# Hybrid S5 and attention encoder block: x and the result moved by position in the chunk, small vectors issued behind the weights

## Chip, cores and metric

The kernel runs on one core of a Trainium2 chip. The metric is device time in microseconds (us) of one execution; the runs of a kernel are told by their median. The profile is one further execution, recorded by the hardware profiler. Engines: PE multiplies matrices, DVE and POOL work elementwise, ACT evaluates functions and copies, and SP issues the transfers (DMA).

## The reference

One layer is computed for a prompt of 512 tokens and a sample of 256, with the same weights:

```
x += 1/2 * postnorm(SwiGLU_1(prenorm(x)))
h  = prenorm(x); z = h @ w_in  -> [u_ssm | q_c | kv_c | k_rope]
y_ssm = groupnorm(S5 bidirectional complex-diagonal SSM(u_ssm) + GLU)
y_att = groupnorm(bidirectional MLA(q_c, kv_c, k_rope))
x += postnorm(concat(y_ssm, y_att) @ w_out)
x += 1/2 * postnorm(SwiGLU_2(prenorm(x)))
```

The model width is 1024, the hidden width 2816, everything in float32. `g_q`, `g_ssm_out`, `b_glu` and `g_att_out` are the small vectors of the mixers.

## The kernel before

The 768 tokens are six tiles of 128. The state-space part works in chunks of 8 tokens, so the kernel keeps tokens in the order of the position j in the chunk: a tile of the prompt (tiles 0 to 3) holds two positions of 64 chunks each, a tile of the sample (4 and 5) four positions of 32 chunks. `runs` (L123) describes such a tile in DRAM, `load_x` (L128) loads it and `store_x` (L132) stores one of the result.

The stages, with the names that the prediction uses:

- **Start** (`run`, `read` L1144, `feed` L1152). Each tile of x is loaded, squared and summed on ACT (`squares`, L151), turned into a factor on POOL (L145, L146), normalised on DVE (L169) and turned by 8 PE transposes (L180); ACT and DVE split the columns into a high and a low part (L92, L93), the blocks B. The first products of the gate weights (L111 to L113, 24 to a group) need the three tiles of the first half of the tokens. `in_order` holds each engine to the order in which this is written.
- **First half-step**, with the state-space setup in the background, up to some 600 us.
- **Way out of the half-step** (`rows` L188, called by `out1` L1169). It takes a tile per step. The tile's row sum of squares (ACT) gives the factor r; DVE scales the tile (L211), POOL adds the residual tile x to it (L212), which `load_x` fetches again, and the sum is stored in a DRAM buffer, x1D. In the next step DVE scales the sum again for the next norm (L215), PE turns it, and so on. Steps are three deep, and each engine is held to the written order: on DVE a step is L211, L215, the two splits, and the two sums of products (L445).
- **Mixers** (`mix` L702): input projection, states, attention.
- **Way out of the mixers** (`mix_out` L1054): the same `rows`, with the residual read from x1D, whose rows lie in the order of the tile, and its result written to x2D.
- **Second half-step and its way out** (`out2` L1174): `rows` again without a next norm, the residual from x2D; `store_x` writes the result, the last tile in two halves of its channels (L232, L233).

All transfers are issued by SP, in one order that the tile scheduler sets. They take eight completion semaphores in turn, so that a transfer is issued when the one eight places before it has landed; a store also waits for the engine that makes its tile, and a load for its buffer.

Of the kernel before, what the change touches and what calls it, by code (L numbers as in the profile page):

```python
# [13 lines left out]
PSUM = bass.MemoryType.PSUM  # L14
# [4 lines left out]
NJ = 8  # L19
# [5 lines left out]
# Tokens lie in the order n = j*64 + k for the j-th token of the prompt's chunk k, then  # L25
# n = 512 + j*32 + k for the sample's. A chunk is 8 tokens.
# [3 lines left out]
# A float32 operand of a matmul is the exact sum of two float32r parts of 12 significant bits;  # L30
# a product is three passes, hi*hi + hi*lo + lo*hi.
#
# Half-step, per pair of 128-wide tiles of the hidden layer: with the weights' blocks A[tile][half
# of the inner dimension] and the tokens' blocks B[half of the inner dimension][half of the tokens],
# the four products of blocks take Winograd's seven multiplications.
# [6 lines left out]
PACE = 1.9  # steps of the setup in the background of each group of products  # L42
BACK = 27  # the unit of attention from which the states' way back goes beside it
WOUT = (35, 36, 37, 38)  # the units at which a row of blocks of w_out is made ready
AHEAD = 3  # how many of its matrices are loaded ahead
# [3 lines left out]
class Kernel:  # L49
# [17 lines left out]
    def load(self, src, shape, name="raw", tile=None):  # L67
        t = (tile or self.w4)(name, shape, F32)
        self.nc.sync.dma_start(t, src)
        return t  # L70

# [3 lines left out]
    # banks of PSUM: 4 for products, 2 for what follows them, 2 that serve a third purpose  # L75
# [19 lines left out]
    def opnd(self, src, eng=None):  # L95
        """[128, 4, 128] of weights as (hi, lo)"""
        t = self.w4("w", [2, 4, 128])
        self.split(t[:, 0], t[:, 1], src, eng)
        return t[:, 0], t[:, 1]

    def wrow(self, src):
        """[128, 1024] of weights as (hi, lo)"""
        h, l = (self.w4("w", [1024]) for _ in range(2))
        self.split(h, l, src)
        return h, l

    def prod(self, ps, A, B, start, stop):
        """ps (+)= A^T B over the four inner tiles of a block"""
        for k in range(4):
            first = start and k == 0  # L110
            self.nc.tensor.matmul(ps, A[0][:, k, :], B[0][:, k, :], start=first, stop=False, skip_group_check=True)  # L111
            self.nc.tensor.matmul(ps, A[0][:, k, :], B[1][:, k, :], start=False, stop=False, skip_group_check=True)  # L112
            self.nc.tensor.matmul(ps, A[1][:, k, :], B[0][:, k, :], start=False, stop=stop and k == 3, skip_group_check=True)  # L113

    def chain(self, ps, pairs):
        """ps = sum over (lhs hi, lhs lo, rhs hi, rhs lo)"""
        for i, (lh, ll, rh, rl) in enumerate(pairs):
            last = i == len(pairs) - 1
            self.nc.tensor.matmul(ps, lh, rh, start=i == 0, stop=False)  # L119
            self.nc.tensor.matmul(ps, lh, rl, start=False, stop=False)  # L120
            self.nc.tensor.matmul(ps, ll, rh, start=False, stop=last)  # L121

    def runs(self, x, t, drams):  # L123
        """the rows of a token tile in DRAM and in x, as [j, chunk, channel]"""
        which, n, j0 = (0, 2, 2 * t) if t < 4 else (1, 4, 4 * t - 16)
        return drams[which][0].rearrange("(k j) d -> j k d", j=NJ)[j0 : j0 + n], x

    def load_x(self, x, t, drams):  # L128
        src, dst = self.runs(x, t, drams)
        self.nc.sync.dma_start(dst, src)  # L130

    def store_x(self, drams, x, t, ch):  # L132
        dst, src = self.runs(x, t, drams)
        self.nc.sync.dma_start(dst[:, :, ch], src)
# [19 lines left out]
    def rms_cols(self, S, n, name):  # L154
        """one factor per token, [128, 6], from sums of squares [128 channels, 768 tokens]"""
        nc = self.nc
        ps = self.dn([128, 8], "ps_r")
        for t in range(NTILE):
            nc.tensor.matmul(ps[:, t : t + 1], S[:, 128 * t : 128 * t + 128], self.ones, start=True, stop=True)
        r = self.small.tile([128, NTILE], F32, name=name)  # L160
        nc.vector.tensor_scalar(r, ps[:, :NTILE], 1.0 / n, EPS, op0=ALU.mult, op1=ALU.add)
        nc.gpsimd.tensor_tensor(r, r, self.mhalf.broadcast_to([128, NTILE]), op=ALU.pow)
        return r

# [1 line left out]
    def normed(self, xn, x, g, spare):  # L166
        """xn = the normalised rows x"""
        r = self.rms_factor([self.sumsq(x, spare)], D)
        self.nc.vector.scalar_tensor_tensor(xn, x, r, g, op0=ALU.mult, op1=ALU.mult)  # L169

    def turn(self, xn, t, bl, bank=None):
        """the rows of a token tile as columns of the blocks bl; returns what takes them out of PSUM"""
        nh, c = t // 3, slice(128 * (t % 3), 128 * (t % 3) + 128)
        banks = []
# [13 lines left out]
    def rows(self, acc, produce, g_post, residual, store, g_pre=None, bl=None):  # L188
        """a sub-layer's way out by tiles of tokens: the last of its products, post-norm and residual, then the
        next one's pre-norm into the blocks bl; in steps, each tile three steps deep. Without a next one, the last  # L190
        tile goes by halves of its channels"""
# [48 lines left out]
    def in_order(self):  # L240
        """each engine takes what is traced here in that order"""
        traced = self.nc.cur_bb.bb.instructions
        n = len(traced)
# [9 lines left out]
    def combos(self, bl, out):  # L253
        """Winograd's sums of the tokens' blocks, in steps"""
# [33 lines left out]
    def group(self, last, calls):  # L288
        """the matmuls of an accumulation group, after the group that was last in its bank"""
# [7 lines left out]
    def behind(self, steps, count=1):  # L297
        """count of steps, their instructions kept behind those that each engine has been given before"""
# [15 lines left out]
    def ffn(self, bl, wnames, way_out, n_plain, feed, lead, background=iter(()), read=lambda nh: None):  # L314
# [6 lines left out]
        # at the start of the kernel GpSimd takes a share  # L321
# [185 lines left out]
    def cmul(self, t, o, a, b, eng):  # L507
        """o = a * b for pairs (re, im); t: a temporary of o's shape"""
# [7 lines left out]
    def ssm_setup(self):  # L516
# [43 lines left out]
        # the angle less its whole turns, in pieces of 2 pi whose products with the turns are exact  # L560
# [22 lines left out]
        # f = (lam_bar - 1) / lam  # L583
# [22 lines left out]
        # the states are kept conjugate, so that a real part is a sum of products  # L606
# [8 lines left out]
        # powers by offset: the forward half 1, lam .. lam^8; the backward half lam^8 .. lam, 1 from offset 1  # L615
# [82 lines left out]
    def chunks(self, dram):  # L698
        """[channels, tokens] as (first chunk, [j, c, g, k]) of the prompt and of the sample"""
        return [(k0, dram[:, a:b].rearrange("(g c) (j k) -> j c g k", c=16, j=NJ)) for k0, a, b in ((0, 0, 512), (64, 512, 768))]  # L700

    def mix(self, bl, before):  # L702
# [6 lines left out]
        def columns(c0, n, tile=self.w4):  # L709
            """n <= 2 tiles of 128 columns of w_in from c0, one at a time"""  # L710
# [3 lines left out]
        def from_h(op, i, nh, done):  # L714
            """their products: done(i, half, psum [128, 384])"""
# [5 lines left out]
        # the state-space inputs u, by way of DRAM to [(j, c), g, chunk]  # L721
# [28 lines left out]
        # chunk inputs of the states: column s of XS gets what enters the state after its chunk s-1,  # L750
        # the backward half in the reversed order of chunks
# [34 lines left out]
        # the queries' latents, times their gain; their norm is a factor per token  # L786
        gq = self.small.tile([128, 3], F32, name="gq")
        nc.sync.dma_start(gq, A["g_q"][0].rearrange("(t p) -> p t", p=128))
# [16 lines left out]
        # keys' and values' latents and the shared rotary key, token by token  # L805
# [29 lines left out]
        # projections of the queries, keys and values  # L835
# [5 lines left out]
        for k in range(3):  # L841
            raw = self.load(A["w_uq"][0, 128 * k : 128 * k + 128, :].rearrange("p (h d) -> p h d", h=8), [8, 96])
            h, l = (self.w4("w", [768]) for _ in range(2))
            # the halves of the rotary channels apart
# [58 lines left out]
        # what the states' way back reads  # L903
# [12 lines left out]
        # attention, by tiles of 128 queries  # L916
        cols = {}
        for nm in ("g_ssm_out", "b_glu"):
            cols[nm] = self.small.tile([128, 4], F32, name=nm)
            nc.sync.dma_start(cols[nm], A[nm][0].rearrange("(t p) -> p t", p=128))  # L920
# [3 lines left out]
        self.bcast(g_att, "g_att_out")  # L924
        # [half of the tokens][hi, lo]
# [8 lines left out]
        # in stages, each some units behind the one before: a unit is a tile of queries with one or two heads  # L934
# [24 lines left out]
        def weigh(u):  # L959
# [10 lines left out]
            if h0 + n == 8:  # L970
# [4 lines left out]
                # the group norm's factor goes with the rows of w_out's product  # L975
# [25 lines left out]
        def ssm_out():  # L1001
            for b in range(AHEAD):
                fetch(b)
            # the backward half back into the order of chunks
# [8 lines left out]
            for b in range(8):  # L1013
# [9 lines left out]
                # twice the tanh-gelu  # L1023
# [30 lines left out]
    def mix_out(self, ohl, ra, cols, wo, res, out_x2, bl):  # L1054
# [31 lines left out]
        for ct in range(4):  # L1086
# [9 lines left out]
            # from the order by j and the chunks of both sequences to that of the tokens  # L1096
# [97 lines left out]
def constants():  # L1194
    """what depends on shapes alone: the identity, rotary tables by position, a diagonal mask"""
# [36 lines left out]
```

## Time and profile before

| what | us |
|---|---|
| median of 3 runs (1571.25 to 1573.25) | 1571.81 |
| span of the profiled execution | 1569.7 |
| median less span | 2.1 |
| PE busy in the span | 1429.2 (91%) |
| DVE busy | 1057.0 (67%) |
| ACT busy | 579.8 (37%) |

A busy share is a mean over stages. The view in forty slices, each of 39 us, shows where PE is not full; the timeline of one engine then shows, behind each instruction that had to wait, how long and for what. The view by stretches gives for each engine its busy time with the number of instructions, then PE's granted clock, the mean share of the 16 DMA engines that were busy, and the rate.

### The profile page before, as it was taken

Reading aid. Unit: us, or ns where it says so; the run is one execution under the profiler, and the core shown is the slowest. Engines: PE = TensorE matmul, PEld = TensorE weight load, DVE = VectorE, ACT = ScalarE, POOL = GpSimd, SP = SyncE. Lnnn points to the kernel's source line nnn. Section 1 sums busy time; section 2 is a strip of 40 time slices with the busy share of each in tenths; the row PEclk is TensorE's granted clock in tenths of the full one; section 3 lists DMA queues with packets and bytes.
Section 4 is the critical chain, followed back from the end, with each engine's and each line's share of the span. In section 5 each row is a group of like instructions: output and inputs, shape, how many; then the busy total and the mean of one; then the engine's idle time right before and its main releaser. Section 6 shows DMA issues by size and latency. Waiting matters only on the chain. (4 is left out here: it accounts for less than half of the span.)

```text
span 1569.7 us, 20564 instructions
## 1 busy us (share of the span) xinstructions
PE 1429.2 (91%) x7868; PEld 1304.9 (83%) x7868; DVE 1057.0 (67%) x1864; ACT 579.8 (37%) x1101; POOL 249.6 (16%) x277
## 2 busy tenths in 40 slices
PE   1698998999999999799979999799999999999990
PEld 0697776999999999699957988598999999999980
DVE  1459689866677765526998555797677766677741
ACT  1323332422233323335646654345333322233410
POOL 0037783000000002401200112431000000000031
PEclk9898999999999999999989999899999999999995
DMA  2532431221222122472202533322222122222131
GB/s 87 153 79 78 141 105 52 81 81 54 81 67 68 56 80 86 173 221 71 58 1 81 149 116 139 121 94 81 59 77 74 61 81 65 70 67 68 54 110 64
DMA packets 115574, 137.52 MB, mean 88 GB/s; under 512 B 31252, under 2 KB 96148, under 8 KB 115476
## 3 DMA queue, kind: packets, MB, share of 16 engines
q1 hardware_dynamic: 115476, 136.21, 27.8%
q8 instruction: 62, 1.02, 0.3%
q14 instruction: 36, 0.29, 0.1%
HBM read 113.44 MB, written 21.95 MB: 86 GB/s over the span
## 5 line engine op out<-in xcount | busy, mean ns | idle before, releaser
L92 ACT CAST w<-raw 128x512 fp32r<-128x512 f32 (+3 forms) x327 | 220.3, 693 | 304.2 <-PE ps_d L120 88.2
L93 DVE TENSOR_TENSOR w<-raw,w 128x512 fp32r<-128x512 f32 (+3 forms) x327 | 256.9, 802 | 68.6 <-ACT w L92 59.4
L445 DVE TENSOR_TENSOR acc<-acc,ps_d 128x512 f32<-128x512 f32 x216 | 146.2, 684 | 115.3 <-PE ps_d L121 114.9
L119 PE MATMUL ps_d<-w,hid 128*128 128x512 f32 x528 | 210.5, 399 | 9.7 <-DVE acc L445 7.2
L120 PE MATMUL ps_d<-w,hid 128*128 128x512 f32 x528 | 210.1, 398 | 0.0
L121 PE MATMUL ps_d<-w,hid 128*128 128x512 f32 x528 | 207.6, 398 | 0.0
L1138 POOL TENSOR_SCALAR g<-g 128x1024 f32<-128x1024 f32 x2 | 5.6, 2778 | 753.8 <-DMA g<-in_g_ffn_post 420.4
L119 PEld LDWEIGHTS ps_d<-w,hid 128*128 128x128 f32 x528 | 100.4, 190 | 29.8 <-DVE acc L445 8.4
L121 PEld LDWEIGHTS ps_d<-w,hid 128*128 128x128 f32 x528 | 100.8, 191 | 21.9
L120 PEld LDWEIGHTS ps_d<-w,hid 128*128 128x128 f32 x528 | 100.7, 191 | 17.0
L392 ACT COPY U<-pa 128x384 f32<-128x384 f32 x36 | 17.3, 482 | 150.4 <-PE pa L113 144.8
L92 ACT CAST hid<-hs 128x384 fp32r<-128x384 f32 x88 | 44.4, 513 | 75.4 <-DVE hs L340 74.8
L145 POOL TENSOR_SCALAR r<-ss 128x1 f32<-128x1 f32 x48 | 20.2, 421 | 247.8 <-ACT ps_o L151 112.9
L180 PE MATMUL ps_t<-ident,x 128*128 128x128 f32 x48 | 11.1, 402 | 48.3 <-DVE x L169 43.0
L93 DVE TENSOR_TENSOR hid<-hs,hid 128x384 fp32r<-128x384 f32 x88 | 47.7, 556 | 5.5 <-ACT hid L92 5.4
L180 PEld LDWEIGHTS ps_t<-ident,x 128*128 128x128 f32 x48 | 8.6, 209 | 50.1 <-DVE x L169 27.6
L111 PE MATMUL pe<-T1h,w 128*128 128x384 f32 x144 | 48.2, 335 | 0.5 <-DVE acc L445 0.5
L113 PE MATMUL pa<-B00h,w 128*128 128x384 f32 x144 | 48.4, 336 | 0.0
L111 PE MATMUL pe<-B11h,w 128*128 128x384 f32 x144 | 48.3, 336 | 0.0
L113 PE MATMUL pe<-B11h,w 128*128 128x384 f32 x144 | 48.3, 336 | 0.0
L113 PE MATMUL pb<-T2h,w 128*128 128x384 f32 x144 | 48.3, 335 | 0.0
L112 PE MATMUL pa<-B00l,w 128*128 128x384 f32 x144 | 48.3, 335 | 0.0
(372 smaller groups left out, 3926.1 us busy)
## 6 DMA issues: line engine op xcount, KB each, us to landing
raw<-in_w_ffn_gate SPq DMA_DIRECT2D x44, 512.0 KB, 3.7
raw<-in_w_ffn_up SPq DMA_DIRECT2D x44, 512.0 KB, 4.0
raw<-in_w_ffn_down SPq DMA_DIRECT2D x44, 512.0 KB, 3.6
x<-in_x_prompt SPq DMA_DIRECT2D x8, 512.0 KB
dO<-ssm_w SPq DMA_DIRECT2D x32, 128.0 KB, 2.0
dM<-ssm_stg SPq DMA_DIRECT2D x16, 256.0 KB, 2.2
raw<-dM SPq DMA_DIRECT2D x8, 512.0 KB, 4.7
raw<-dO SPq DMA_DIRECT2D x8, 512.0 KB, 3.6
```

Source lines behind the costliest of these rows:

```text
L92: self.nc.scalar.copy(hi, src)
L93: (eng or self.nc.vector).tensor_tensor(lo, src, hi.bitcast(F32), op=ALU.subtract)
L111: self.nc.tensor.matmul(ps, A[0][:, k, :], B[0][:, k, :], start=first, stop=False, skip_group_check=True)
L112: self.nc.tensor.matmul(ps, A[0][:, k, :], B[1][:, k, :], start=False, stop=False, skip_group_check=True)
L113: self.nc.tensor.matmul(ps, A[1][:, k, :], B[0][:, k, :], start=False, stop=stop and k == 3, skip_group_check=True)
L119: self.nc.tensor.matmul(ps, lh, rh, start=i == 0, stop=False)
L120: self.nc.tensor.matmul(ps, lh, rl, start=False, stop=False)
L121: self.nc.tensor.matmul(ps, ll, rh, start=False, stop=last)
L145: nc.gpsimd.tensor_scalar(r, ss[0], 1.0 / n, EPS, op0=ALU.mult, op1=ALU.add)
L180: self.nc.tensor.transpose(banks[kh][:, k, :], xn[:, (4 * kh + k) * 128 : (4 * kh + k + 1) * 128], self.ident)
L392: nc.scalar.copy(U2, pa)
L445: tt(acc[:, t, sl], acc[:, t, sl], ps, op=ALU.add)
```

## The change

A tile of x or of the result was one transfer whose DRAM side has the position outermost, then the chunk, then the channel. Now each position is a transfer of its own, from 64 (prompt) or 32 (sample) rows of DRAM to as many partitions. A tile is two or four transfers. The small vectors go through a new `late`, which puts the transfer behind the weight load that was written last, in the order that the scheduler keeps.

```
     def load(self, src, shape, name="raw", tile=None):
         t = (tile or self.w4)(name, shape, F32)
-        self.nc.sync.dma_start(t, src)
+        self.loaded = self.nc.sync.dma_start(t, src)
         return t
+
+    def late(self, dst, src):
+
+        order = mybir.DependencyInfo(mybir.DependencyClass.NoSync, mybir.DependencyReason.DATA)
+        i = self.nc.sync.dma_start(dst, src)
+        self.tc.add_manual_dep(i.ins, self.loaded.ins.name, order, reason="late")
...
     def runs(self, x, t, drams):
-        """the rows of a token tile in DRAM and in x, as [j, chunk, channel]"""
         which, n, j0 = (0, 2, 2 * t) if t < 4 else (1, 4, 4 * t - 16)
-        return drams[which][0].rearrange("(k j) d -> j k d", j=NJ)[j0 : j0 + n], x
+        rows, k = drams[which][0].rearrange("(k j) d -> j k d", j=NJ), 128 // n
+        return [(rows[j0 + i], x[k * i : k * i + k]) for i in range(n)]
 
     def load_x(self, x, t, drams):
-        src, dst = self.runs(x, t, drams)
-        self.nc.sync.dma_start(dst, src)
+        for src, dst in self.runs(x, t, drams):
+            self.nc.sync.dma_start(dst, src)
 
     def store_x(self, drams, x, t, ch):
-        dst, src = self.runs(x, t, drams)
-        self.nc.sync.dma_start(dst[:, :, ch], src)
+        for dst, src in self.runs(x, t, drams):
+            self.nc.sync.dma_start(dst[:, ch], src)
...
-        nc.sync.dma_start(gq, A["g_q"][0].rearrange("(t p) -> p t", p=128))
+        self.late(gq, A["g_q"][0].rearrange("(t p) -> p t", p=128))
...
-            nc.sync.dma_start(cols[nm], A[nm][0].rearrange("(t p) -> p t", p=128))
+            self.late(cols[nm], A[nm][0].rearrange("(t p) -> p t", p=128))
...
-        self.bcast(g_att, "g_att_out")
+        self.late(g_att, A["g_att_out"][0, :].partition_broadcast(128))
```

The instructions of PE, DVE, ACT and POOL keep their order; only SP's list differs. At the start, SP before (the loads of x with the gain and the first weights):

```order
L130 DMA x<-in_x_prompt 128x1x1024
L137 DMA g<-in_g_ffn_pre 128x1024
L1150 DMA ident<-in_c_ident 128x128
L130 DMA x<-in_x_prompt 128x1x1024 x2
L69 DMA raw<-in_w_ffn_gate 128x4x256 x2
L788 DMA gq<-in_g_q 128x3x1
L920 DMA g_ssm_out<-in_g_ssm_out 128x4x1
L920 DMA b_glu<-in_b_glu 128x4x1
L137 DMA g_att<-in_g_att_out 128x512
L130 DMA x<-in_x_prompt 128x1x1024
L130 DMA x<-in_x_sample 128x1x1024 x2
L69 DMA raw<-in_w_ffn_up 128x4x256 x2
```

SP now, at the same place:

```order
L138 DMA x<-in_x_prompt 64x1024 x2
L145 DMA g<-in_g_ffn_pre 128x1024
L1158 DMA ident<-in_c_ident 128x128
L138 DMA x<-in_x_prompt 64x1024 x4
L69 DMA raw<-in_w_ffn_gate 128x4x256 x2
L138 DMA x<-in_x_prompt 64x1024 x2
L69 DMA raw<-in_w_ffn_up 128x4x256 x2
L138 DMA x<-in_x_sample 32x1024 x8
```

The four small vectors have left the place between the gate weights and the fourth tile, and the weights `up` now stand ahead of the sample's tiles. In the mixers, SP before (`qT` takes the rotated queries, `T` matrices of the states):

```order
L69 DMA raw<-in_w_uq 128x768 x3
L69 DMA raw<-in_c_ropeq 128x768 x2
L69 DMA raw<-in_w_ukv 128x1024 x2
L870 DMA qT<-rot 16x768 x16
L912 DMA T<-dK 16x8x128 x8
```

SP now, at that place:

```order
L69 DMA raw<-in_w_uq 128x768 x3
L69 DMA raw<-in_c_ropeq 128x768 x2
L69 DMA raw<-in_w_ukv 128x1024 x2
L75 DMA g_ssm_out<-in_g_ssm_out 128x4x1
L75 DMA b_glu<-in_b_glu 128x4x1
L75 DMA g_att<-in_g_att_out 128x512
L878 DMA qT<-rot 16x768 x16
L920 DMA T<-dK 16x8x128 x8
```

Three of the vectors stand behind the last weight load of the projections and ahead of the transfers of the rotated queries; the fourth, `gq`, stands ahead of the first load of the part of `w_in` for the keys (`raw<-in_w_in 128x3x288`). At the end, SP before (`x2D` holds the residual):

```order
L1175 DMA x<-x2D 128x1024
L134 DMA out<-x 2x64x1024 x2
L134 DMA out<-x 4x32x1024
L134 DMA out<-x 4x32x512 x2
L1218 UNCONDITIONAL_BRANCH
```

And now:

```order
L1183 DMA x<-x2D 128x1024
L142 DMA out<-x 64x1024 x4
L142 DMA out<-x 32x1024 x4
L142 DMA out<-x 32x512 x8
L1226 UNCONDITIONAL_BRANCH
```

Five issues have become sixteen, in the same place and order.

## Rows read from the trace of the kernel before

**Rows 1.** The page: PE's busy tenths in forty slices of the span
```profile
PE   1698998999999999799979999799999999999990
```

**Rows 2.** Stretches: engines' busy us and counts, PE clock, DMA share, GB/s
```profile
8.00:10.00 2.00, 0.00 (x0) 0.00 (x0) 0.00 (x0) 0.00 (x0) 0.00 (x0) 1.00 0.13 53
600.00:605.00 5.00, 5.00 (x30) 4.96 (x30) 3.26 (x6) 1.25 (x3) 2.77 (x1) 1.00 0.87 294
894.00:895.00 1.00, 1.00 (x12) 1.00 (x11) 1.00 (x3) 0.08 (x1) 0.29 (x1) 1.00 0.85 182
```

**Rows 3.** Timeline of SP at the start: start, us, issue, count
```profile
2.45 9.60 SPq L130 DMA_DIRECT2D x<-in_x_prompt  x2
12.09 14.66 SPq L69 DMA_DIRECT2D raw<-in_w_ffn_gate  x2
```

**Rows 4.** Timeline of ACT at the start; in brackets the idle time and its end
```profile
13.70 1.06 ACT L151 ACTIVATE squares<-x 128x1024 f32<-128x1024 f32 x1 [11.70 <-DMA x<-in_x_prompt]
...
36.08 1.06 ACT L151 ACTIVATE squares<-x 128x1024 f32<-128x1024 f32 x1 [8.27 <-DMA x<-in_x_prompt]
64.11 0.62 ACT L92 CAST w<-raw 128x512 fp32r<-128x512 f32 x1 [5.02 <-DMA raw<-in_w_ffn_up]
```

**Rows 5.** Timeline of PE: first product, and first of the third group
```profile
41.37 0.69 PE L111 MATMUL ps<-B00h,w 128*128 128x384 f32 x1
69.91 0.67 PE L111 MATMUL ps<-B00h,w 128*128 128x384 f32 x1
```

**Rows 6.** Stretches behind it, columns as in the second group
```profile
70.00:72.00 2.00, 2.00 (x9) 2.00 (x8) 1.16 (x1) 2.00 (x5) 0.72 (x2) 0.50 0.43 79
80.00:90.00 10.00, 10.00 (x60) 10.00 (x59) 4.49 (x7) 4.62 (x9) 4.59 (x1) 1.00 0.33 33
```

**Rows 7.** Timelines of DVE, POOL and PE in the first way out
```profile
630.30 1.28 DVE L215 SCALAR_TENSOR_TENSOR y<-x,r,g 128x1024 f32<-128x1024 f32 x1 [0.72 <-POOL r L146]
640.34 1.28 DVE L215 SCALAR_TENSOR_TENSOR y<-x,r,g 128x1024 f32<-128x1024 f32 x1 [0.71 <-POOL r L146]
...
635.00 2.40 POOL L212 TENSOR_TENSOR x<-x,y 128x1024 f32<-128x1024 f32 x1 [4.73 <-DMA x<-in_x_prompt]
...
651.64 1.94 PE L180 MATMUL ps_t<-ident,y 128*128 128x128 f32 x8 [6.06 <-DVE y L215]
```

**Rows 8.** Timelines of DVE and POOL in the mixers' way out
```profile
993.90 3.38 DVE L215 SCALAR_TENSOR_TENSOR y<-x,r,g 128x1024 f32<-128x1024 f32 x1 [0.71 <-POOL r L146]
1003.97 3.40 DVE L215 SCALAR_TENSOR_TENSOR y<-x,r,g 128x1024 f32<-128x1024 f32 x1 [0.70 <-POOL r L146]
...
1003.90 2.39 POOL L212 TENSOR_TENSOR x<-x,y 128x1024 f32<-128x1024 f32 x1
```

**Rows 9.** The end: timelines of SP and POOL, and the last stretch with transfers
```profile
1524.29 26.86 SPq L134 DMA_DIRECT2D out<-x  x5
...
1538.85 1.74 POOL L233 TENSOR_TENSOR x<-x,y 128x512 f32<-128x512 f32 x1 [2.32 <-DMA x<-x2D]
...
1568.00:1569.00 1.00, 0.00 (x0) 0.00 (x0) 0.00 (x0) 0.00 (x0) 0.00 (x0) 0.50 0.04 16
```

**Rows 10.** SP's timeline, two issues (KB, us to landing), the vectors' readers
```profile
892.54 4.02 SPq L1037 DMA_DIRECT2D dY<-yy  x8
...
699.59 0.40 SPq L69 DMA_DIRECT2D raw<-in_w_in  x1
...
dY<-yy SPq DMA_DIRECT2D x16, 96.0 KB, 2.4
...
gq<-in_g_q SPq DMA_DIRECT2D x1, 1.5 KB, 12.1
...
712.03 0.58 ACT L794 ACTIVATE qcT<-ps,gq 128x384 fp32r<-128x384 f32 x1
...
749.11 2.43 SPq L69 DMA_DIRECT2D raw<-in_w_ukv  x2
...
764.56 0.27 POOL L921 TENSOR_SCALAR g_ssm_out<-g_ssm_out 128x4 f32<-128x4 f32 x1
```

## Prediction, made before the changed kernel was run

> **What bounds the kernel now.** I read the slices of the page first [rows 1]: PE is at nine tenths or more nearly throughout, so an edit pays only where PE is not full, and there are three such places that this change touches. In the first two slices PE is at 1 and 6 tenths; in the seventeenth, around 640 us, at 7; in the last at 0. Everywhere else the edit can only shift what follows.
>
> At the start ACT waits for one tile of x after another [rows 4]: tile 0 is squared at 13.70 us and tile 2 at 36.08, 11.2 us to a tile, after 11.70 and 8.27 us of idling that a load of x ends. The stretch from 8 to 10 us [rows 2] says why: only x is moving, at 53 GB/s, and the DMA share is 0.13, which is 2 of 16 engines. A tile has 524 kB, so it takes 9.9 us, about the distance of the squares. The other loads are caught in it: SP stands for 9.60 us on two issues of x and for 14.66 us on the gate weights [rows 3], and the weights `up` reach ACT at 64.11 us [rows 4]. PE has its first product at 41.37 and the first of its third group at 69.91 [rows 5]; from there it is full (in ten microseconds of the second row of [rows 6], 10.00 us busy).
>
> In the first way out the residual tiles come again by the slow transfers: POOL's sum waits 4.73 us for x, DVE's L215 comes every 10.04 us (630.30 to 640.34), and PE waits 6.06 us to turn a tile [rows 7].
>
> At the end the result leaves by the slow transfers: SP stands 26.86 us on five stores, and POOL's last sum waits 2.32 us for a residual tile behind them. It is done at 1538.85 + 1.74 = 1540.59, yet data moves until about 1568.3 [rows 9]. Some 28 us of the span are nothing but stores.
>
> **Rate of the pieces.** The trace of before has no transfer of 64 or 32 rows of 4 KB, so its rate has to be bounded. Loads over all 128 partitions move 294 GB/s [rows 2]; stores from 16 partitions, as fast as SP issued them, move 182 GB/s at a DMA share of 0.85 [rows 2], so few partitions do not confine a transfer to two engines. I take 240, between the two, since 64 rows are nearer to neither, and keep 182 and 294 for the range.
>
> The Trainium skill speaks against this change: SBUF — State Buffer, "Door 1: The DMA port swizzle (why `[64,N]` ≈ `[32,N]`)", gives 196 GB/s for 64 partitions against 328 for 128, and "Can I just issue two DMAs to hit both halves?" says that the halves serialize. By that the start's term would be about 37 us in place of the one below. Its comparison is with a whole tile that all engines share, which is not what the trace shows before.
>
> **The start.** Data moves from 2 us, and tile 0 was there at 13.70, so a landing is seen 13.70 - 2 - 9.9 = 1.8 us after its data. Now x0, the gain, the identity, x1 and x2 are 2.2 MB, then come 1.05 MB of gate weights, 0.52 of x3, 1.05 of `up`, and x4, x5. With x at 240 and the rest at 294 GB/s: x2 is there at 2 + 6.6 + 2.0 + 1.8 = 12.4 us, the gate weights at 16, `up` at 21.7, x4 at 24. Issue is no limit: a 262 kB piece takes 1.1 us to move, and SP's small pieces take 4.02 / 8 = 0.50 us each [rows 10]. From the square of x2 to the first product passed 41.37 - 36.08 = 5.3 us [rows 4, 5], work of ACT, POOL, DVE and PE that stays; the gate's two casts lie in it and would wait about 1 us. So PE starts at 12.4 + 5.3 + 1 = 18.7 us. Two groups of 24 products and two turnings of a tile lie ahead of the third group: at 6 products per us (60 in 10 us, clock 1.00) a group takes 4 us, at 4.5 per us (9 in 2 us, clock 0.50) 5.3 [rows 6]. The first at the slow clock, with 2 x 1.5 us of turning: 5.3 + 4 + 3 = 12.3, so the third group begins at 31 us, and no load is later than that. That is 69.91 - 31 = 39 us. PE came to its third group after a pause and ran it at clock 0.50 [rows 6]; coming without one saves up to 2 us more. With x at 182 GB/s the third group begins at 33.5, with 294 at 30. I take **-39.5 us**, range 36 to 42. What follows is full on PE, so it is all kept.
>
> **The first way out.** Here the wait for x goes, and I ask what is late next. The mixers' way out runs the same `rows` with a residual whose transfers are not slow, and there L215 comes at 993.90 and 1003.97: every 10.07 us [rows 8]. So the wait is not the bound there. L215 takes 3.40 us, not 1.28: POOL's sum L212 begins 0.07 us before it and both run at once, and it ends 1.08 us after POOL does (1007.37 against 1006.29). In the first way out POOL's sum came late because of x, so it never met L215. With x in time both are freed by the same factor on POOL, as in the mixers' way out, and they collide: the wait for x is replaced by one for POOL. By the period of 10.07, less 0.1 for the shorter sums L445, tiles keep coming every 10 us, and each L215 ends 2 us later than now; the fourth tile's, which PE waits for at 651.64, by about 3 us. I take half a microsecond off for the pauses further on, in which PE can catch up: **+2.5 us**, bounds -6 (below, the first rival) and +3.5.
>
> **The end.** The last residual tile is no longer late, so POOL and DVE are done at about 1539.5, not 1540.6. The eight pieces of the last tile then need eight issues of 0.50 us: 1543.5; the last was issued at 1543.0 and lands 2.4 us later, as the pieces of dY of 96 KB do [rows 10], at about 1545.4. After the last data came 1569.7 - 1568.3 = 1.4 us. The span ends at 1546.8, or **-23 us**; with issues of 0.40 us 24, with 0.65 us 21.5.
>
> **The small vectors.** Their four issues leave the start, where they cost what is in the sum already. `gq` is issued at what was 699.59 us, in front of a load of `w_in`; its first reader, L794, ran at 712.03. It took 12.1 us to land among the loads of x [rows 10], and would be there at 711.7 even so. The other three come after 749.11 + 2.43 = 751.5 us, SP has nothing else until POOL's L868 and L921 at 764.56, and 12.1 us from 751.6 is 763.7 [rows 10]. Nothing: 0, bounds 0 and +3 if they are pressed further.
>
> **Sum.** 1569.7 - 39.5 + 2.5 - 23 = 1509.7 of span; the median stands 2.1 us above the span of the profiled run, which gives 1511.8, say **1512 us**. By the bounds: -42 - 6 - 24 gives 1500, -36 + 3.5 + 3 - 21.5 gives 1521.
>
> **Rivals.** *DVE goes first.* If L215 begins before POOL's sum in the first way out, it keeps its 1.28 us, POOL does the waiting, and the period falls by 3.40 - 1.28 = 2.1 us to 8: at the fourth tile PE is let go some 5 to 6 us earlier than now, not 2.5 later. Time 1503.5. The 0.07 us between the two are little, but in [rows 8] POOL was first, and L215 took 3.38 and 3.40 us. The Trainium skill (SBUF — State Buffer, "Who interferes with whom") says of the two engines' common port that issue order decides who blocks; the row with POOL first agrees.
>
> *The vectors come late.* If `gq` lands 5 us behind its first reader, ACT holds a product's bank for so long and PE stops: 1512 + 5 = 1517. For it speaks that only 0.3 us are left at 12.1; against it, that those 12.1 us were spent behind the slow loads, which are gone.
>
> *The pieces go through the same two engines one after another.* Then a tile still takes 9.9 us, and only the order at the start and the extra issues differ: 1572, no change.
>
> *Slower: a piece goes through a single engine*, since it is that engine's share of rows. One of two engines at 53 GB/s moves 26.5, so a tile in two such pieces takes 19.8 us: the start loses 3 x 9.9 = 30 us, the first way out some 40, the six tiles at the end some 60: about 1700. It decides from 53 GB/s: a piece must be below that to lose. Against it stand the 182 GB/s from 16 partitions.
>
> **How the numbers follow.** The forecast 0.80, DVE first 0.10, vectors late 0.05, same two engines 0.02, single engine 0.03. The range 1500 to 1521 holds the first three with their bounds and leaves out the last two; some of the 0.80 may lie beyond its bounds, in terms of the start above all, and with that about 2 in 10 are left out. A measurement of this kernel tells about 0.2% from no change; faster by more 0.95, within 0.02, slower by more 0.03.
>
> **What would show it.** In the changed kernel's profile: the squares of x2 at 11 to 14 us and PE's third group at 30 to 34; in the first way out L215 of 3.4 us beside POOL's L212, and about 10 us between tiles; stores that end within 8 us of the last sum; no wait of L794 or L921 for a DMA. The forecast is wrong by most if a tile of x takes longer than 3 us, or if L215 stays at 1.28 us.

## The result, and the profile after

The changed kernel takes **1506.8 us** (median of 4 runs, 1504.82 to 1512.25) against 1571.5 for the kernel before (4 runs, 1569.49 to 1573.25): a ratio of 0.960, with a 95% interval of 0.958 to 0.962. The forecast was 1512 us with a range of 1500 to 1521. The profiled run has a span of 1505.6 us against 1569.7, so 64.1 us are to be accounted for.

The page's slices after (busy tenths of PE, 40 slices of 37.6 us), which answer to [rows 1]:

```profile
span 1505.6 us, 20640 instructions
PE   6988979999999999799979999799999999999996
PEclk9999999999999999999989999999999999999999
```

The start's first slice is now at 6 tenths and the last at 6; the seventeenth, the first way out, stays at 7.

**The start.** SP's issues (SPq), ACT and PE in the order of time; the columns are start and busy time in us, queue or engine, line, operation, output and input, count, and in brackets the idle time ahead and what ended it. This answers to [rows 3 to 5]:

```profile
0.72 1.24 SPq L138 DMA_DIRECT2D x<-in_x_prompt  x2
3.10 2.39 SPq L138 DMA_DIRECT2D x<-in_x_prompt  x4
5.53 1.14 SPq L69 DMA_DIRECT2D raw<-in_w_ffn_gate  x2
9.46 1.43 SPq L69 DMA_DIRECT2D raw<-in_w_ffn_up  x2
...
5.48 1.28 ACT L159 ACT_TABLE_LOAD   x1 [5.48 <-DMA x<-in_x_prompt]
10.59 1.06 ACT L159 ACTIVATE squares<-x 128x1024 f32<-128x1024 f32 x1 [2.67 <-DMA x<-in_x_prompt]
13.12 1.06 ACT L159 ACTIVATE squares<-x 128x1024 f32<-128x1024 f32 x1 [0.32 <-DMA x<-in_x_prompt]
...
18.35 0.69 PE L117 MATMUL ps<-B00h,w 128*128 128x384 f32 x1
31.69 0.42 PE L117 MATMUL ps<-B00h,w 128*128 128x384 f32 x1
```

The six pieces of x0 to x2 are issued by 5.5 us, x2 is squared at 13.12 instead of 36.08 us, the gate weights are issued right behind, and PE has its first product at 18.35 and the first of its third group at 31.69 (41.37 and 69.91 before).

**The first way out.** POOL's residual sum (L220, L212 before) and DVE's L223 (L215 before) in the order of time; this answers to [rows 7]:

```profile
602.49 2.34 POOL L220 TENSOR_TENSOR x<-x,y 128x1024 f32<-128x1024 f32 x1
...
602.56 3.35 DVE L223 SCALAR_TENSOR_TENSOR y<-x,r,g 128x1024 f32<-128x1024 f32 x1 [0.71 <-POOL r L154]
612.48 3.35 DVE L223 SCALAR_TENSOR_TENSOR y<-x,r,g 128x1024 f32<-128x1024 f32 x1 [0.71 <-POOL r L154]
```

PE's waits between 571 and 660 us (us in total, times, longest):

```profile
PE ps_t L188 <- DVE y L223: 11.7, 4, 6.1
```

POOL no longer waits for x. It begins 0.07 us ahead of DVE, L223 takes 3.35 us instead of 1.28, tiles come every 9.92 us, and PE still waits up to 6.1 us to turn one.

**The end.** DVE's last sums, POOL's last sum and SP's last issues; this answers to [rows 9]:

```profile
1494.32 0.69 DVE L453 TENSOR_TENSOR acc<-acc,ps_d 128x512 f32<-128x512 f32 x1 [0.68 <-PE ps_d L127]
1498.49 1.63 DVE L241 TENSOR_TENSOR x<-x,y 128x512 f32<-128x512 f32 x1
...
1497.93 1.65 POOL L241 TENSOR_TENSOR x<-x,y 128x512 f32<-128x512 f32 x1 [0.92 <-issue]
...
1490.11 13.27 SPq L142 DMA_DIRECT2D out<-x  x14
```

Two stretches behind them (stretch and its length, busy time of PE, PEld, DVE, ACT and POOL, PEclk, DMA share, GB/s):

```profile
1503.00:1504.00 1.00, 0.00 (x0) 0.00 (x0) 0.00 (x0) 0.00 (x0) 0.00 (x0) 0.50 0.54 150
1504.00:1505.00 1.00, 0.00 (x0) 0.00 (x0) 0.00 (x0) 0.00 (x0) 0.00 (x0) 0.50 0.15 43
```

The last sum ends at 1500.12, the last issue at 1503.38, data moves until about 1505, and the span ends at 1505.6. DVE and POOL collide here too: DVE's L241 begins 0.56 us after POOL's and takes 1.63 us. In the kernel before it began 0.07 us ahead of POOL's sum of [rows 9] and took 0.69:

```profile
1538.78 0.69 DVE L233 TENSOR_TENSOR x<-x,y 128x512 f32<-128x512 f32 x1 [0.81 <-DMA x<-x2D]
```

**Where the 64 us came from.** PE runs the same 7868 matmuls in the same order in both kernels and in every experiment below, so the start of its n-th matmul can be compared. Worked out from the records of the profiled executions, in us:

```
stretch (numbers of PE's matmuls)                before   after  difference
start to no. 2900, ahead of the first way out     598.8   559.1     -39.7
2900 to 3300, first way out                        87.1    90.4      +3.3
3300 to 4970, mixers                              272.7   272.9      +0.2
4970 to 5460, mixers' way out                     115.1   111.9      -3.2
5460 to 7860, second half-step                    458.1   458.1       0.0
7860 to the end of the span                        37.9    13.3     -24.6
```

Three rows are the terms of the prediction. The fourth, -3.2, is none of them, and is taken up below.

### The profile page after: what moved, and what is told of

Its sections match the earlier page's. It is cut to its first block, busy times and chain, and to the rows that moved or that the text cites. A ratio compares the mean times of both kernels' runs of the same rounds, so it can differ in the third digit from the quotient of the medians.

```text
span 1505.6 us, 20640 instructions
## 1 busy us (share of the span) xinstructions
PE 1424.6 (95%) x7868; PEld 1301.2 (86%) x7868; DVE 1067.1 (71%) x1864; ACT 579.2 (38%) x1101; POOL 251.7 (17%) x277
## 5 line engine op out<-in xcount | busy, mean ns | idle before, releaser
L153 POOL TENSOR_SCALAR r<-ss 128x1 f32<-128x1 f32 x48 | 20.9, 436 | 223.6 <-ACT ps_o L159 113.5
L117 PE MATMUL pe<-T1h,w 128*128 128x384 f32 x144 | 48.7, 338 | 1.8 <-DVE acc L453 1.8
L344 ACT ACTIVATE hs<-hs 128x384 f32<-128x384 f32 x54 | 28.3, 526 | 53.1 <-DVE hs L430 39.2
L118 PE MATMUL pe<-T1l,w 128*128 128x384 f32 x144 | 48.7, 339 | 0.0
L119 PE MATMUL pe<-T1h,w 128*128 128x384 f32 x144 | 48.7, 338 | 0.0
```

Of the source, the lines that this page charges most:

```text
L153: nc.gpsimd.tensor_scalar(r, ss[0], 1.0 / n, EPS, op0=ALU.mult, op1=ALU.add)
L344: nc.scalar.activation(hs[:, i, half(nh)], ps, AF.Silu)
```

## Experiments

The theory: the start's and the end's gain are the faster pieces alone; the small vectors do nothing; in the first way out the wait for x was replaced by the collision of POOL and DVE. The rivals: the vectors carry part of the start, x was the true bound of the way out, or the collision costs nothing.

The kernel before was run again beside the experiments: its median was 1571.8 us beside the first three and the residual tiles in one transfer, 1570.4 beside the pieces cut in two, DVE first, the table load and the second queue, and 1569.6 beside the two kernels with two edits. So a microsecond or two between the times of two experiments says nothing.

### The start's tiles in one transfer each again

```diff
-                    self.load_x(xs[t], t, X)
+                    src, dst = self.whole(xs[t], t, X)   # all of the tile, as [j, chunk, channel]
+                    nc.sync.dma_start(dst, src)
```

> The changed kernel, but the six tiles of x at the start move as one transfer each again, with the chunk's position outermost; the small vectors stay behind the weight loads. Theory A (the start's gain is all in the pieces): the third group begins at 66 to 70 us as before, time 1506.8 + 35 to 39 = 1542 to 1546 us. Theory B (in the kernel before SP stood 10.6 us on the issues of the four vectors, 26.80 to 37.35 us, ahead of x3 and of the weights up, which PE's third group waits for; their move alone gives back about that): up is issued at about 32 instead of 42.86 us, the third group begins at about 59 us, time 1506.8 + 28 = 1535 us.

Measured: 1546.27 us (1545.05 to 1548.92). SP and PE at the start:

```profile
12.11 14.75 SPq L69 DMA_DIRECT2D raw<-in_w_ffn_gate  x2
26.90 5.56 SPq L1160 DMA_DIRECT2D x<-in_x_prompt  x1
32.51 8.72 SPq L1160 DMA_DIRECT2D x<-in_x_sample  x2
41.27 10.97 SPq L69 DMA_DIRECT2D raw<-in_w_ffn_up  x2
...
68.09 0.67 PE L117 MATMUL ps<-B00h,w 128*128 128x384 f32 x1
```

Theory A holds. Without the vectors SP stands nearly as long, now on the tiles of x (14.3 us where it stood 10.6 on the vectors and some 5 on x): its issues stand as long as slow transfers are ahead of them. The weights `up` are issued 1.6 us earlier than before, and the third group begins 1.8 us earlier. From the start to no. 2900 it takes 597.7 us, 38.6 more than after the change. So the pieces carry the start, and the vectors' place is worth under 2 us while x is slow.

### The small vectors at the start again

```diff
-        self.late(gq, ...)
+        nc.sync.dma_start(gq, ...)        # and so for g_ssm_out, b_glu, g_att
```

> The changed kernel, but the four small vectors are issued at the start again, between the gate weights and the fourth tile of x. Theory A (without slow transfers of x they cost only their four issues, some 2 us, ahead of a load that nothing waits for): the third group begins at 31.7 to 33 us, time 1507 to 1509 us. Theory B (they hold SP, since gq's elements of 4 bytes are slow to land and each issue waits for the one eight places earlier): the weights up come 4 to 8 us later, the third group begins at 36 to 40 us, time 1511 to 1515 us.

Measured: 1506.39 us (1505.44 to 1508.59), no difference from 1506.80. SP issues them from 8.08 to 13.09 us, `up` at 14.29 instead of 9.46 us, and PE has its first product at 18.08; matmul no. 80, just ahead of the third group, starts at 31.2 us against 30.9. Theory A holds: with fast pieces the vectors cost some 5 us of a queue that nobody waits for.

### The result's tiles in one transfer each again

```diff
-        for dst, src in self.runs(x, t, drams):
-            self.nc.sync.dma_start(dst[:, ch], src)
+        dst, src = self.whole(x, t, drams)
+        self.nc.sync.dma_start(dst[:, :, ch], src)
```

> The changed kernel, but the result's tiles are stored as one transfer each again. Theory (the end's term is the stores alone): what lies between the last sum of acc and the end of the span grows from 10.6 us to about 35 us, time 1506.8 + 24.5 = 1531 us, 1529.5 to 1533; nothing ahead of 1440 us moves. Rival (part of the end's gain came from the residual tiles of the last way out, which are loaded on the same queue): the same stores cost over 26 us.

Measured: 1530.96 us (1530.34 to 1534.07), 24.2 more. SP's stores and POOL's last sum:

```profile
1483.32 31.15 SPq L146 DMA_DIRECT2D out<-x  x5
1497.97 1.74 POOL L245 TENSOR_TENSOR x<-x,y 128x512 f32<-128x512 f32 x1 [2.31 <-DMA x<-x2D]
```

A stretch near the end, in which tiles of the sample are stored, four positions each (columns as for the end above):

```profile
1510.00:1520.00 10.00, 0.00 (x0) 0.00 (x0) 0.00 (x0) 0.00 (x0) 0.00 (x0) 0.50 0.23 87
```

From no. 7860 to the end it takes 37.9 us, as in the kernel before, and POOL's wait for the last residual tile behind the stores is back with 2.31 us. The end's term is the stores alone.

### Each piece cut in two

```diff
-        return [(rows[j0 + i], x[k * i : k * i + k]) for i in range(n)]
+        h = k // 2
+        return [(rows[j0 + i, h * z : h * z + h], x[k * i + h * z : k * i + h * z + h])
+                for i in range(n) for z in range(2)]
```

> The changed kernel with every piece cut in two again: 32 rows of the prompt, 16 of the sample. Theory (a piece of few rows still spreads over the engines, and what counts is one issue on SP per piece): at the start the first product comes 1 to 3 us later, at the end 16 issues lie behind the last sum instead of 8, 3 to 4 us more: time 1506.8 + 6 = 1513 us, 1510 to 1515. Rival (fewer rows mean fewer engines and a lower rate): a tile of x takes over 4 us, the third group begins after 37 us, time over 1518 us.

Measured: 1512.89 us (1509.5 to 1516.75). From no. 7860 to the end it takes 16.9 us instead of 13.3, which is eight more issues of 0.45 us each. The first product comes at 18.77 us, which is no later: in the changed kernel and the six experiments that leave the start alone it comes at 18.3 to 19.5. A piece of 32 KB lands 1.7 us after its issue, like one of 64. Between 21 and 25 us, when SP issues pieces of 16 rows of the sample, 0.55 of the 16 engines are busy. So 16 rows still spread, and the price of a piece is its issue, where issues are what ends last. That the time comes out at the 1513 foretold is in part luck: the start gave nothing of its 1 to 3 us, while the mixers' way out took 3.3 us more in this execution, as it does in others (see below).

### The residual tiles of the first way out in one transfer each again

```diff
-                return self.rows(acc, product, g_post, lambda x, t: self.load_x(x, t, X),
+                return self.rows(acc, product, g_post, lambda x, t: nc.sync.dma_start(*self.whole(x, t, X)[::-1]),
```

> The changed kernel, but the residual tiles of the first way out are loaded as one transfer each again; start and end stay as in the changed kernel. Theory (the wait for x was only replaced by DVE's L223 and POOL's L220 running at once, 3.4 us instead of 1.28): POOL's sum waits some 4.7 us for x again, L223 takes 1.28 us again, the period stays 10 us, and the time is 1506.8 - 2.6 = 1504 us, 1503 to 1507.5. Rival (the wait for x held up the way out): time 1511 to 1517 us.

Measured: 1504.88 us (1502.05 to 1510.54). The runs overlap with those of the changed kernel, so the time alone says only that nothing is lost; the trace says why. POOL's sum waits for x again, and L227 (L223 of the changed kernel) is short again:

```profile
593.61 2.39 POOL L224 TENSOR_TENSOR x<-x,y 128x1024 f32<-128x1024 f32 x1 [4.72 <-DMA x<-in_x_prompt]
603.49 2.36 POOL L224 TENSOR_TENSOR x<-x,y 128x1024 f32<-128x1024 f32 x1 [4.57 <-DMA x<-in_x_prompt]
598.95 1.28 DVE L227 SCALAR_TENSOR_TENSOR y<-x,r,g 128x1024 f32<-128x1024 f32 x1 [0.72 <-POOL r L158]
```

The stretch from no. 2900 to 3300 takes 87.1 us, to the tenth what it took before the change; it takes 89.6 to 90.4 in the changed kernel and in the five experiments (of the start, the vectors, the stores, the table and the second queue alone) that leave this way out as it is. The rival is out by 6 us and more.

### DVE first

One tiny instruction on POOL, ahead of the residual sum; it comes 12 times, in the first way out and in the mixers' (the last way out, which the expectation names too, has no L223 and does not get it):

```diff
                     r_u = self.rms_factor([self.sumsq(X[u], Y[u])], D)
+                    pool.tensor_scalar(self.pad, self.pad, 1.0, None, op0=ALU.mult)   # [128, 1], times one
```

> The changed kernel with one tiny instruction on POOL (a multiplication of one number per row by one, about 0.2 us) between the row factor and the residual sum L220, in all three ways out; the order on every engine is otherwise the same. In the changed kernel POOL's L220 begins 0.06 to 0.07 us before DVE's L223, so 0.2 us is enough to turn their order round. Theory (who begins first decides, and the collision is what the first way out's 46.9 us between matmul 2900 and 3300 hang on, against 43.0 before the change): L223 takes 1.28 us, L220 some 3.4 us, the first way out gives back 3 to 5 us, the mixers' way out as much: time 1506.8 - 7 = 1500 us, 1497 to 1503. Rival (the later residual sum becomes the bound, or L223 is slowed all the same): 1506 to 1509 us.

Measured: **1495.23 us** (1492.76 to 1498.16), all runs under all of the changed kernel's. POOL and DVE in the first way out:

```profile
598.60 0.22 POOL L213 TENSOR_SCALAR pad<-pad 128x1 f32<-128x1 f32 x1
598.78 3.41 POOL L220 TENSOR_TENSOR x<-x,y 128x1024 f32<-128x1024 f32 x1
...
598.65 1.28 DVE L223 SCALAR_TENSOR_TENSOR y<-x,r,g 128x1024 f32<-128x1024 f32 x1 [0.72 <-POOL r L154]
606.53 1.28 DVE L223 SCALAR_TENSOR_TENSOR y<-x,r,g 128x1024 f32<-128x1024 f32 x1 [0.72 <-POOL r L154]
```

PE's waits from 571 to 651 us:

```profile
PE ps_t L188 <- DVE y L223: 4.1, 1, 4.1
```

Now DVE begins 0.13 us ahead, keeps its 1.28 us, and POOL takes 3.41. Tiles come every 7.88 us instead of 9.92. The first way out takes 80.6 us (-9.8), the mixers behind it 276.2 (+3.3) and the mixers' way out 107.2 (-4.7). In the last kernel below, whose code is the same up to there, the three take 82.9, 272.8 and 108.4 us, so how much comes at once and is given back differs by execution; first way out and mixers together gain 6.5 and 7.6 us. The sum that POOL is late with has slack, the row that DVE is late with has none. The Trainium skill (SBUF — State Buffer, "Who interferes with whom") says that a DVE instruction with two inputs in SBUF, as L223 has in x and g, contends with a POOL instruction that reads SBUF, that their common port pair is an exclusive lock, and that issue order decides who blocks. The trace agrees to 0.2 us: in the changed kernel L223 ends 1.08 us after L220 did, here L220 ends 2.26 us after L223 did, and alone they take 1.28 and 2.4.

### DVE first, with the residual tiles in one transfer each

Both edits above together.

> The kernel of e5_dve_first (one tiny POOL instruction, so that L223 begins ahead of L220), but the residual tiles of the first way out are loaded as one transfer each again. Theory (two limits of about 10 us stood one behind the other in the first way out, the slow tile of x with 9.9 us and the collision; the pieces take away the first, the tiny instruction the second, and either alone gains nothing there): tiles come every 9.9 to 10 us again instead of 7.9, POOL waits some 2 to 5 us for x, and PE loses what it gained there: time 1495.2 + 5 = 1500 us, 1499 to 1503. Rival (the form of the residual loads does not matter at all): 1495 us.

Measured: 1501.11 us (1499.22 to 1502.9). POOL waits 3.4 to 4.7 us for x, and the second and third tile come 10.1 us apart:

```profile
595.55 2.40 POOL L224 TENSOR_TENSOR x<-x,y 128x1024 f32<-128x1024 f32 x1 [4.74 <-DMA x<-in_x_prompt]
605.65 2.40 POOL L224 TENSOR_TENSOR x<-x,y 128x1024 f32<-128x1024 f32 x1 [4.56 <-DMA x<-in_x_prompt]
```

The four corners of the first way out, from no. 2900 to 3300:

```
                       residual tiles whole    in pieces
POOL first                    87.1 us           90.4 us
DVE first                     90.0 us           80.6 us (82.9 in the last kernel below)
```

Two limits of about 10 us a tile stood one behind the other. Taking away either alone gains nothing. In the lower left corner there is no collision to turn round: POOL's sum comes late because of x and takes 2.40 us, and the DVE row (L227 here) takes 1.28, as in the upper left. Both together gain 4.2 to 6.5 us there. Part of it can be given back in the mixers: from no. 2900 to 4970 the corners read 359.8, 363.3, 362.8 and 356.8 us (355.7 in the last kernel), a gain of 3.0 to 4.1. Why the lower left corner is 2.9 us above the upper left is open.

### The table load early, and the last stores on a second queue

Two smaller edits, each on the changed kernel. A tiny square ahead of all else on ACT brings its table load forward:

```diff
+            nc.scalar.activation(const("warm", [1]), self.ones, AF.Square)
```

> The changed kernel with one tiny square on ACT ahead of everything, so that the table load (1.28 us, which in the changed kernel follows the arrival of the first tile, at 5.48 us) comes while x is still on its way. Theory (the table load lies on the way of tile 0 only, while x2 and the gate weights set the first product): the first square comes 1.3 us earlier, the first product at 18.3 us or up to 1 us earlier, time 1505.8 to 1506.8 us. Rival (ACT's chain from the first square sets the first product): 1.3 us off, 1505.5 us.

Measured: 1509.94 us (1506.34 to 1514.79), no gain. The first square came at 5.55 us instead of 6.77, but the second at 12.23 instead of 10.59, and the first product at 19.88. ACT waited for x1, which landed later; the profiled execution was the slowest of the five. Whether the edit did that or the run is not settled: the seven kernels with the start of the changed kernel square x1 at 10.59 to 11.42 us, and their third group begins at 29.7 to 32.5, in this one at 32.5.

The four last pieces on ACT's queue:

```diff
+        queue = self.nc.scalar if ch.start else self.nc.sync
         for dst, src in self.runs(x, t, drams):
-            self.nc.sync.dma_start(dst[:, ch], src)
+            queue.dma_start(dst[:, ch], src)
```

> The changed kernel, but the four pieces of the second half of the last tile are issued on ACT's queue instead of SP's. Theory (behind the last sum the end is bound by the issues, one after another on SP at 0.5 us): SP has four issues behind the last sum, ACT four beside them, the span ends 1.3 to 2 us earlier, time 1505 us. Rival (the transfers or the landing bind): no change, 1506.8 us.

Measured: 1507.84 us (1506.56 to 1509.21). From no. 7860 to the end it takes 12.2 us instead of 13.3, so the issues were the bound there, but a gain of 1.1 us does not show in the time. On top of DVE first it was tried again:

> The kernel of e5_dve_first with the last four pieces of the result on ACT's queue, as in e10_end_act. In e10_end_act the stretch from the last sum of acc to the end of the span was 9.5 us instead of 10.6. Theory (the two gains lie in different places and add up): 1494 us, 1492 to 1495. Rival (the end's microsecond is lost in the spread of the runs): 1495 us.

Measured: **1494.2 us** (1492.74 to 1495.01), the fastest of all, a ratio of 0.952 (0.950 to 0.953) to the kernel before; the stretch at the end is 12.2 us again. Its runs overlap with those of DVE first alone, and the kernel before was 0.8 us faster beside it, too: the ratios are the same, 0.952. That the two gains add up is shown for the stretch at the end alone.

## Why the prediction was right, step by step

**Start**, -39.5 foretold, -39.7 measured. x2 squared at 13.12 us (11 to 14 foretold), first product at 18.35 (18.7), third group at 31.69 (31). 38.2 us are there at the third group, the rest in that group itself: it takes 5.0 us to the next, where it took 6.6 and ran its first two microseconds at granted clock 0.50 [rows 6]; now it comes without a pause, at 1.00. That the sum meets the measurement to 0.2 us is luck. Within it, x2 is squared 0.7 us later than reckoned (12.4), the 1 us for the gate's casts does not come (5.2 us from the square to the first product), and from there to the third group it takes 13.3 us, not 12.3. And the seven kernels with this start (three with one more memset on POOL) begin their third group at 29.7 to 32.5 us and reach no. 2900 after 556.5 to 559.7. The rate taken was 240 GB/s; in the first way out, where only pieces of x are left in the queue (two w_in loads ahead of them were issued by 561.4 us and land in a median of 5.2), it reads

```profile
567.00:568.00 1.00, 1.00 (x7) 0.96 (x6) 0.28 (x2) 0.70 (x2) 0.00 (x0) 1.00 1.06 250
568.00:569.00 1.00, 1.00 (x8) 0.99 (x6) 1.00 (x2) 0.34 (x1) 0.00 (x0) 1.00 1.01 238
569.00:571.00 2.00, 1.60 (x7) 0.91 (x6) 1.85 (x5) 1.03 (x2) 0.00 (x0) 1.00 1.05 246
```

in the last two columns: all engines busy, 238 to 250 GB/s. The Trainium skill gives 196 GB/s for 64 partitions (SBUF — State Buffer, "Door 1: The DMA port swizzle (why `[64,N]` ≈ `[32,N]`)") and says that transfers to the two halves serialize ("Can I just issue two DMAs to hit both halves?"); that is not what these rows show.

**First way out**, +2.5 foretold, +3.3 measured, within the bounds (+2.5 to +3.3 in the kernels that share it). The mechanism stood in the prediction with its place and its size: L223 of 3.35 us (3.4 foretold), a period of 9.92 (about 10), POOL first by 0.07 us. The fourth tile lost 4.0 us (no. 2900 to 3094: 43.0 before, 47.0 after) where about 3 was foretold, and 0.7 came back, where half a microsecond was.

**End**, -23 foretold, -24.6 measured; the term was mis-sized by 1.6 us. The last sum is done 5.1 us after the last sum of `acc`, 0.9 earlier than before (1.1 foretold): the late residual is gone, but DVE's sum collides with POOL's, which the working did not have. Behind it the working had 7.3 us, 4.0 for eight issues and 3.3 from there to the end; it was 5.5: the issues end 3.26 us behind the last sum, since POOL's half was done 0.54 us before DVE's, and 2.3 us follow, because a piece of 64 KB lands 1.7 us after its issue, not 2.4 as the 96 KB of dY.

**Small vectors**, 0 foretold, 0 measured, both at their readers (`gq` lands 2.5 us after its issue at 661.3 and is first read at 674.9; no engine waits for any of the four) and, by the experiment, at the start.

**What was no term**: the -3.2 us in the mixers' way out. That way out's code is the same in all these kernels but for the tiny instruction, and those without it take two values. The whole stretch (columns as above, PEclk third from the end) in the kernel before:

```profile
958.60:1073.70 115.10, 101.10 (x492) 88.85 (x491) 91.64 (x88) 50.47 (x89) 47.90 (x39) 0.93 0.31 107
```

In the changed kernel:

```profile
922.30:1034.20 111.90, 99.24 (x492) 87.39 (x492) 91.53 (x88) 50.26 (x89) 46.56 (x39) 0.95 0.30 108
```

In the one with the last stores on ACT's queue:

```profile
920.00:1035.10 115.10, 101.03 (x493) 89.12 (x492) 91.56 (x88) 50.28 (x89) 46.56 (x39) 0.93 0.30 105
```

The third is the changed kernel's own code there, at the time of the kernel before. Of the nine kernels without the tiny instruction four take 111.8 to 112.0 us, all at a mean granted clock of 0.95, and five, the kernel before among them, 115.0 to 116.0, all at 0.93. So the 3.2 us go with the clock that an execution was granted there, and not with the change. What decides between the two is open. Without them the span would be 1508.8, 0.9 below the foretold 1509.7: the end's 1.6 and the start's 0.2, less the way out's 0.8 and 0.2 in the mixers, but for rounding.

**The rival DVE goes first** was priced at 8.5 us below the forecast and given a chance of 0.10. It did not happen, but it was 0.07 us away, and the tiny instruction made it happen. The first way out was priced at -6 us against the kernel before and measured -6.5 (-4.2 in the last kernel). That is -9.8 us against the changed kernel there, -6.5 with the mixers behind it, and another -4.7 us came in the mixers' way out, which the price had left out.

## What to carry to other kernels

Look at the DMA share while a slow transfer moves: 2 of 16 engines meant here that its outermost dimension had 2 entries, and cutting it so that rows stand outermost costs one issue a piece and gave back 40 us at the start and 25 at the end. Where a wait is taken away, look for the next limit of the same size in a place that runs the same code without that wait; here it was read from the mixers' way out beforehand, and it took the whole gain. When two engines collide on every tile, see which of them has slack, and let the other begin first: 0.2 us of delay on POOL gave 11.6 us.

## What the runs showed of the hardware

The engines that a transfer keeps busy follow its outermost dimension here: a DMA share of 0.13 (2 of 16) and 53 GB/s with two positions [rows 2], 0.25 (4 of 16) and 91 GB/s with four (stores of the sample's tiles in the kernel before, 1549 to 1560 us), and 1.01 to 1.06 (all of them) and 238 to 250 GB/s with pieces of 64 rows.

An issue on SP is short by itself (0.6 us for a piece of 64 rows at the start) but stands while slow transfers are ahead of it: with slow tiles in flight the two gate weights took SP 14.75 us, without them 1.14. The rule of the eight completion semaphores does not explain this. In the kernel before, the 9.60 us on two issues of x and the 14.66 us on the gate weights [rows 3] are the fourth to seventh transfers, ahead of which no issue stands eight places earlier; what they wait for inside the queue is not shown. So a slow transfer holds up issues that have nothing to do with it, and taking a small one out of the queue only lets the next one wait in its place.

Executions of the same code differ in three places here, the start (third group at 29.7 to 32.5 us), the mixers' way out (111.8 to 116.0 us in the kernels without the tiny instruction) and the stretch of the setup (no. 600 to 1200, 110.6 to 113.5 us), while the second half-step takes 458.1 us in every one. An edit worth 1 to 3 us is therefore read from its own stretch, not from the time.
